# Where the modulation's partial sums are folded: from TensorE to GpSimd and VectorE

## The chip, the core and the metric

The kernel runs on one NeuronCore of a Trainium2 chip, as one program. The metric is the device time of one execution in microseconds; of several runs the median is given. The engines are named as the profile names them: PE (TensorE matmuls), PEld (TensorE's weight loads, which overlap PE), DVE (VectorE), ACT (ScalarE), POOL (GpSimd) and SP (SyncE, which here only issues DMAs).

## The reference, cut to what matters

The network is a diffusion transformer of two layers on 256 latent tokens and 256 context tokens of width 1024, one retention layer and one neighbourhood-attention layer, each followed by an MLP. Every layer is modulated: a vector `c` (and `c_ctx` for the context) is multiplied by a 1024 x 6144 matrix, and the product is cut into six pieces, shift, scale and gate for the mixer and for the MLP.

```
silu_c = silu(c); silu_cc = silu(c_ctx)
for i in range(2):
    mod   = silu_c  @ ada_w[i] + ada_b[i]        # 1024 -> 6144, for the latents
    mod_c = silu_cc @ ada_w[i] + ada_b[i]        # the same for the context
    sh1, sc1, g1, sh2, sc2, g2 = split(mod, 6)
    h = x * (1 + sc1) + sh1
    y = mixer(h)                                 # retention (i=0), neighbourhood attention (i=1)
    x = layer_norm(ALPHA * x + g1 * y)
    h = x * (1 + sc2) + sh2
    x = layer_norm(ALPHA * x + g2 * mlp(h))      # and the same for the context where i=0
```

The change touches only how `mod` and `mod_c` are finished, for all pieces but the first shift and scale of layer 0.

## The kernel before, in words

All large products run on PE with float32 operands split in a high and a low part (`hi`, `lo`), three matmuls for each product. The work is one long sequence of stages: an opening (projection of the first retention head, together with the first modulation, which PE computes itself), four retention heads (0 to 3), the first MLP in two halves, then the second layer: neighbourhood attention and its MLP. Weights are streamed from DRAM by SP into the pool `rawp` (tiles `raw`, `rawa` for the modulation's matrix; four buffers for both), ACT rounds them (`hi`), DVE subtracts (`lo`).

The later modulation is a background task, `bg_stream`. It has ten parts, named (layer, which modulation, part): parts 0 and 1 are two halves of shift and scale ("columns"), part 2 is the gate. In order: (0,0,2), (0,1,0), (0,1,1), (0,1,2), (1,0,0), (1,0,1), (1,0,2), (1,1,0), (1,1,1), (1,1,2). For each part eight pieces of the matrix are loaded, DVE multiplies each with a column of silu(c) and adds up per partition (`weigh`, in `strips` in layer 0's parts and in `acc` later), and `folded` reduces that on DVE with a transposing reduction into a small tile `red`: 128 partitions by 32 columns for each of the `nt` token kinds. What is left are four groups of 32 partitions that have to be added. `nt` is 2 where the context needs its own modulation, and 1 in the parts (1,0,2) and (1,1,0) to (1,1,2).

That last addition is the subject. It is put in the list `due` and run by `flush` at the next background step: `ada_columns` for parts 0 and 1, `ada_gate` for part 2. Before the change PE does it: a matmul of `red` with the constant `fold` (a 128 x 32 matrix that is one where the partition modulo 32 equals the column), into a bank of PSUM that the program calls `pada`. For columns there are four such matmuls, one for each quarter of the output partitions, and DVE adds the bias on the way out into `mods`. For a gate there is one; DVE transposes the result, adds the bias, which POOL has fetched by DMA into the tile `gate`, and POOL writes the row to DRAM (`grow`) by DMA, from where SP or ACT load it later broadcast over the partitions (`load_gate`, tile `G`). The scratch `gate` is one of the eight tiles of the pool `scp` (`scr`).

`mods` is read by `fold`, which combines it on POOL with the layer norm's weights (`AB`, three small instructions). The first reader of (0,1) is the end of head 3, that of (1,0) the end of the first MLP, that of (1,1) the end of the attention.

Instructions are written in program order, but the Tile framework's scheduler sets the order on each engine from its own costs, except where `InOrder` pins an engine (`pe.on`, `dve.on` and so on). POOL is mostly free; it also does the row statistics' power (`rstd`), the products `gs`, the accumulation into the residual `R` and the issue of its own DMAs. Every engine runs its instructions strictly in the order shown, so an instruction that waits holds up all behind it.

Of the kernel before, what the change touches and what calls it, by code (L numbers as in the profile page):

```python
# [10 lines left out]
F32 = mybir.dt.float32  # L11
# [6 lines left out]
P = 128  # L18
# [86 lines left out]
def kernel(  # L105
# [23 lines left out]
    pe, act, dve, pool, sp = (  # L129
        InOrder(tc, getattr(nc, e), e in PIN)  # L130
        for e in ("tensor", "scalar", "vector", "gpsimd", "sync")
    )
# [3 lines left out]
    smp = ec(tc.tile_pool(name="smp", bufs=4))  # L136
# [15 lines left out]
    def nm(s):  # L152
        uid[0] += 1
        return f"{s}_{uid[0]}"

    def bank(s="ps"):
        return psp.tile([P, 512], F32, tag="ps", name=nm(s))
# [5 lines left out]
    def scr(s, dt=F32):  # L163
        return scp.tile([P, 512], dt, tag="scr", name=nm(s))
# [138 lines left out]
    def cv(name, p0=0, p1=P):  # L303
        o, w = CONST_COLS[name]
        if o < NC0:
            return cst0[p0:p1, o : o + w]
        return cst1[p0:p1, o - NC0 : o - NC0 + w]
# [59 lines left out]
    mods = {}  # L367
# [62 lines left out]
    def folded(red, acc, t, c0, n):  # L430
# [3 lines left out]
            axis=mybir.AxisListType.X, op=ALU.add, apply_transpose=True,  # L434
        )

    def ada_columns(l, w, red, c0, nt):

        pr = bank("pada")
        for j in range(4):  # L440
            pe.matmul(
                pr[32 * j : 32 * j + 32, 0 : 8 * nt],
                lhsT=cv("fold"),
                rhs=red[:, :nt].rearrange("p t (k j) -> p j (t k)", j=4)[:, j],
                start=True,
                stop=True,
                tile_position=(0, 32 * j),
            )
        dve.tensor_add(
            out=mods[l, w][:, :, c0 : c0 + 4, :],  # L450
            in0=(
                pr[:, 0:16].rearrange("p (t s k) -> p s k t", t=2, s=2)
                if nt == 2
                else pr[:, 0:8].rearrange("p (s k) -> p s k", s=2).unsqueeze(3).broadcast_to([P, 2, 4, 2])
            ),
            in1=acol[:, COLUMNS.index((l, w)), :, c0 : c0 + 4].unsqueeze(3).broadcast_to([P, 2, 4, 2]),
        )

    def ada_gate(l, w, red, nt):

        tmp = scr("gate")[0:32, :]
        bias, tot, row = tmp[:, 0:32], tmp[:, 64 : 64 + 32 * nt], tmp[:, 128 : 128 + 32 * nt]
        g = (3 * w + 2) * D
        pool.dma_start(out=bias, in_=ada_b[l][g : g + D].rearrange("(b i) -> b i", i=32))
        pr = bank("pada")
        pe.matmul(
            pr[0:32, 0 : 32 * nt], lhsT=cv("fold"), rhs=red[:, :nt].rearrange("p t b -> p (t b)"),
            start=True, stop=True, tile_position=(0, 0),
        )
        dve.transpose(out=tot, in_=pr[0:32, 0 : 32 * nt])  # L470
        dve.tensor_add(
            out=row.rearrange("p (t i) -> p t i", t=nt), in0=tot.rearrange("p (t i) -> p t i", t=nt),
            in1=bias.unsqueeze(1).broadcast_to([32, nt, 32]),
        )
        for t in range(nt):
            pool.dma_start(
                out=grow[l, w][t].rearrange("(b i) -> b i", i=32), in_=row[:, 32 * t : 32 * t + 32]
            )
# [26 lines left out]
    def bg_stream():  # L505
# [13 lines left out]
        for step, (l, w, part, offs, n) in enumerate(plan):  # L519
# [28 lines left out]
            if n == KC - 1:  # L548
                if part < 2:
                    due.append(lambda a=(l, w, red, 4 * part, nt): ada_columns(*a))  # L550
                else:
                    due.append(lambda a=(l, w, red, nt): ada_gate(*a))
# [324 lines left out]
    def part_v(k, a, b):  # L877
# [8 lines left out]
        out=lgn[:, 0], in_=ret_decay[0].rearrange("(o d) h -> o (d h)", o=1).broadcast_to([P, 8])  # L886
# [19 lines left out]
    w = ws[0]  # L906
# [98 lines left out]
    for h in range(RH):  # L1005
# [9 lines left out]
        else:  # L1015
# [15 lines left out]
            for u in range(4):  # L1031
                ((wh, wl),) = take(1)
                for t in range(4):
                    for kk in range(2):
                        k = 2 * u + kk
# [72 lines left out]
        for t in range(4):  # L1108
            po = bank("po")
            scs = list(range(4)) if t < 2 else [2, 3]  # L1110
            for i, sc in enumerate(scs):
                a, b = S[sc]
# [8 lines left out]
                out=on, in0=po[:], scalar1=mv[:, 0:1], scalar2=r[:], op0=ALU.subtract, op1=ALU.mult  # L1121
# [51 lines left out]
        else:  # L1173
# [11 lines left out]
            def proj(t, half):  # L1185
                return gated(tok_mm(t, half, wus[half]), t, half, G1)
# [4 lines left out]
            def turn(t):  # L1191
                return [mod_pt(xns[t], half) for half in range(2)]
# [16 lines left out]
            tmp = proj(1, 1)  # L1209
# [10 lines left out]
            tmp = proj(2, 1)  # L1220
# [56 lines left out]
    for hf in range(2):  # L1277
# [65 lines left out]
        for half in range(2):  # L1343
# [39 lines left out]
            def settle(t):  # L1383

                add_to(t, 1, gated(pb[t], t, 1, G2), dve)
                stat(t, 1)
                return moments(t)
# [14 lines left out]
            m = settle(0)  # L1402
# [5 lines left out]
            m = settle(1)  # L1408
            mm2(2, 4, held[0])
            p = turn(0)  # L1410
# [7 lines left out]
            m = settle(2)  # L1418
            mm2(3, 4, held[0])
            p = turn(1)  # L1420
# [299 lines left out]
    m = settle(3)  # L1720
# [123 lines left out]
    n = NS - 1  # L1844
# [373 lines left out]
```

## Time and profile before

| | us |
|---|---|
| median of 3 runs | 1178.11 |
| lowest, highest run | 1176.97, 1178.76 |
| the profiled execution | 1180.28 |
| its span in the profile | 1178.2 |
| PE busy, share of the span | 1168.4, 99% |
| DVE busy | 846.6, 72% |
| ACT busy | 482.0, 41% |
| POOL busy | 212.9, 18% |
| granted TensorE clock, mean | 0.998 |

The span runs from the first to the last instruction; 2.1 us of the profiled execution's time lie outside it. PE's busy time counts overlapping instructions once and its ends are modelled; so the starts of successive matmuls say more than their lengths. In the rows of a timeline the columns are start, busy time, engine, line, operation, output<-inputs, shapes, how many instructions are merged in the row, and in brackets how long the engine had been idle and what ended it. Almost all rows have line 84, which is the helper that issues each instruction; tiles' names tell them apart. The profile shows each of the kernel's folding matmuls as two records, since their operands are plain float32.

### The profile page before, as it was taken

How to read it: one execution, taken by the hardware profiler on the slowest of the kernel's cores; microseconds unless marked ns; L12 is line 12 of the kernel's file. 1: busy time of each engine (PE TensorE's matmuls, PEld its weight loads, DVE VectorE, ACT ScalarE, POOL GpSimd, SP SyncE). 2: the span in 40 equal slices, each digit the busy share in tenths (PEclk: the TensorE clock that was granted, in tenths of full speed). 3: DMA queues.
4: the chain of work that ended last, by engine and by line, in shares of the span. 5: the costliest groups of instructions: out<-in, count | busy, mean ns of one | idle time of the engine just before them, and what ended most of it. 6: DMA issues, size and time to landing. Idle time of an engine off the chain costs nothing.

```text
span 1178.2 us, 17591 instructions
## 1 busy us (share of the span) xinstructions
PE 1168.4 (99%) x6743; PEld 985.0 (84%) x6743; DVE 846.6 (72%) x1351; ACT 482.0 (41%) x819; POOL 212.9 (18%) x364
## 2 busy tenths in 40 slices
PE   9999999999999999999999999999999999999997
PEld 7788888888888889888888888889888878999886
DVE  3887677777888787757767675678576688876446
ACT  3643332232323246341113332137466576665341
POOL 0103001000200241770203000223344430000001
PEclk9999999999999999999999999999999999999999
DMA  9942544544355426756556665647244434765661
GB/s 279 273 143 93 158 146 146 156 144 143 126 170 170 149 59 218 184 110 212 179 183 211 202 207 187 192 140 212 76 144 126 123 123 151 224 197 189 230 213 38
DMA packets 140115, 195.10 MB, mean 166 GB/s; under 512 B 9936, under 2 KB 81136, under 8 KB 140032
## 3 DMA queue, kind: packets, MB, share of 16 engines
q1 hardware_dynamic: 131904, 182.03, 49.6%
q0 software_dynamic: 6976, 9.39, 3.9%
q10 hardware_dynamic: 1152, 2.56, 0.8%
q8 instruction: 53, 0.87, 0.3%
q14 instruction: 30, 0.25, 0.1%
HBM read 189.12 MB, written 5.75 MB: 165 GB/s over the span
## 4 chain that ended last, share of the span: by engine, by line
PE 97%; DVE 1%; ACT 1%; issue 0%; DMA 0%; POOL 0%; DVEq 0%; ACTq 0%
PE p L84 44%; PE pq L84 8%; PE pv L84 8%; PE pg L84 7%; PE pw L84 7%; PE pn L84 5%; PE pnv L84 4%; PE po L84 3%; PE ppt L84 2%; PE pnw L84 1%; PE pS L84 1%; PE pav L84 1%; PE pada L84 1%; PE pqk L84 1%; PE pt L84 1%; PE p1t L84 1%
## 5 line engine op out<-in xcount | busy, mean ns | idle before, releaser
L84 ACT CAST hi<-raw 128x1024 fp32r<-128x1024 f32 (+2 forms) x228 | 232.7, 1032 | 310.9 <-PE p L84 124.3
L84 DVE TENSOR_TENSOR lo<-raw,hi 128x1024 fp32r<-128x1024 f32 (+2 forms) x228 | 274.0, 1213 | 106.2 <-ACT hi L84 105.7
L84 PE MATMUL p<-hi,hid 128*128 128x512 f32 (+1 forms) x780 | 239.0, 386 | 0.0
L84 PEld LDWEIGHTS p<-hi,hid 128*128 128x128 f32 x780 | 145.7, 188 | 29.5
L84 PE MATMUL p<-hTh,lo 128*128 128x256 f32 (+1 forms) x512 | 166.9, 329 | 0.0
L84 PE MATMUL p<-hTl,hi 128*128 128x256 f32 (+1 forms) x512 | 166.9, 329 | 0.0
L84 PE MATMUL p<-hTh,hi 128*128 128x256 f32 (+1 forms) x512 | 164.0, 330 | 0.0
L84 PE MATMUL p<-lo,hid 128*128 128x512 f32 (+1 forms) x390 | 150.5, 386 | 0.0
L84 DVE SCALAR_TENSOR_TENSOR acc<-rawa,scol,acc 128x1024 f32<-128x1024 f32 x56 | 74.6, 1342 | 65.5 <-DMA rawa<-in_ada_w_dram 65.5
L84 PEld LDWEIGHTS p<-hTh,lo 128*128 128x128 f32 x512 | 96.4, 188 | 8.8
L84 PEld LDWEIGHTS p<-hTl,hi 128*128 128x128 f32 x512 | 96.5, 188 | 8.6
L84 PEld LDWEIGHTS p<-hTh,hi 128*128 128x128 f32 x512 | 95.1, 190 | 8.7
L84 PEld LDWEIGHTS p<-lo,hid 128*128 128x128 f32 x390 | 73.3, 188 | 14.5
L84 DVE SCALAR_TENSOR_TENSOR strips<-rawa,scol,strips 128x512 f32<-128x512 f32 x112 | 78.6, 762 | 0.0
L84 ACT CAST hid<-r 128x256 fp32r<-128x256 f32 (+1 forms) x64 | 31.9, 500 | 106.9 <-DVE r L84 106.9
L84 POOL TENSOR_TENSOR rstd<-rstd,misc 128x1 f32<-128x1 f32 x28 | 19.1, 685 | 213.6 <-DVE rstd L84 212.6
L84 POOL TENSOR_TENSOR R<-R,acc 128x512 f32<-128x512 f32 x16 | 25.9, 1635 | 169.8 <-DVE acc L84 169.7
L84 ACT ACTIVATE s<-s,mn 128x512 f32<-128x512 f32 x64 | 45.5, 713 | 22.0 <-DVE mn L84 22.0
L84 PE MATMUL pw<-hi,oh 128*128 128x512 f32 x128 | 51.0, 398 | 0.0
L84 PE MATMUL pg<-hi,hTh 128*128 128x512 f32 x128 | 50.6, 395 | 0.0
L84 PE MATMUL pw<-hi,ol 128*128 128x512 f32 x128 | 50.0, 390 | 0.0
L84 PE MATMUL pg<-hi,hTl 128*128 128x512 f32 x128 | 49.9, 390 | 0.0
(238 smaller groups left out, 2279.8 us busy)
## 6 DMA issues: line engine op xcount, KB each, us to landing
raw<-in_mlp_w_dram SPq DMA_DIRECT2D x128, 512.0 KB, 4.4
rawa<-in_ada_w_dram SPq DMA_DIRECT2D x80, 512.0 KB, 3.9
raw<-in_ret_w_in_dram SPq DMA_DIRECT2D x42, 512.0 KB, 4.0
raw<-in_nat_w_in_dram SPq DMA_DIRECT2D x24, 512.0 KB, 4.5
rawq<-in_ada_w_dram SPq DMA_DIRECT2D x16, 512.0 KB, 6.1
raw<-in_ret_w_o_dram SPq DMA_DIRECT2D x16, 512.0 KB, 3.5
bias<-rpb_rows POOLq DMA_DIRECT2D x32, 128.0 KB, 2.9
raw<-in_nat_w_o_dram SPq DMA_DIRECT2D x8, 512.0 KB, 3.9
```

Of the source, the lines that this page charges most:

```text
L84: r = f(*args, **kwargs)
```

## The change

The four groups of 32 partitions are added by two copies and two additions (`strip_sums`): partitions 64 to 127 are copied beside partitions 0 to 63 and added, then 32 to 63 beside 0 to 31. For columns POOL does it, four more POOL copies spread the sums to the four quarters of `mods`, and a POOL addition adds the bias. For gates DVE does it, and its transpose then reads `red` and no PSUM. The scratch (`far`, `gate`) moves from `scr` into the tile `row` of the opening, of which there is one.

```diff
+    def strip_sums(red, nt, far, eng):
+        far = far[:, : 32 * nt].rearrange("p (t b) -> p t b", t=nt)
+        for n in (64, 32):
+            eng.tensor_copy(out=far[0:n], in_=red[n : 2 * n, :nt])
+            eng.tensor_add(out=red[0:n, :nt], in0=red[0:n, :nt], in1=far[0:n])
+        return red[0:32, :nt]
+
     def ada_columns(l, w, red, c0, nt):
-        pr = bank("pada")
+        far = smp.tile([P, 256], F32, tag="row", name=nm("far"), bufs=1)
+        tot = strip_sums(red, nt, far, pool).rearrange("p t (s k j) -> p j s k t", s=2, j=4)
+        m = mods[l, w][:, :, c0 : c0 + 4, :]
         for j in range(4):
-            pe.matmul(
-                pr[32 * j : 32 * j + 32, 0 : 8 * nt],
-                lhsT=cv("fold"),
-                rhs=red[:, :nt].rearrange("p t (k j) -> p j (t k)", j=4)[:, j],
-                start=True, stop=True, tile_position=(0, 32 * j),
-            )
-        dve.tensor_add(
-            out=mods[l, w][:, :, c0 : c0 + 4, :],
...
+            pool.tensor_copy(
+                out=m[32 * j : 32 * j + 32], in_=tot[:, j] if nt == 2 else tot[:, j].broadcast_to([32, 2, 4, 2])
+            )
+        pool.tensor_add(
+            out=m, in0=m,
             in1=acol[:, COLUMNS.index((l, w)), :, c0 : c0 + 4].unsqueeze(3).broadcast_to([P, 2, 4, 2]),
         )

     def ada_gate(l, w, red, nt):
-        tmp = scr("gate")[0:32, :]
+        tmp = smp.tile([P, 256], F32, tag="row", name=nm("gate"), bufs=1)
...
-        pr = bank("pada")
-        pe.matmul(
-            pr[0:32, 0 : 32 * nt], lhsT=cv("fold"), rhs=red[:, :nt].rearrange("p t b -> p (t b)"),
-            start=True, stop=True, tile_position=(0, 0),
-        )
-        dve.transpose(out=tot, in_=pr[0:32, 0 : 32 * nt])
+        dve.transpose(out=tot, in_=strip_sums(red, nt, tmp[:, 192:], dve).rearrange("p t b -> p (t b)"))
```

On PE the ten places lose their matmuls and nothing else changes its place. On DVE and POOL the scheduler orders some instructions anew. Three places follow, with before first.

DVE in head 1, between the projection of the values and the scores, where the gate (0,0,2) is finished. `red_953` is the part's reduced sum, `lo_1607` a weight's low part, `vl` the low part of the head's values read out of the banks `pv`, `strips` the running sums of the next part:

```order
L84 TENSOR_TENSOR lo_1575<-raw_1572,hi_1574 128x1024
L84 TENSOR_TENSOR lo_1607<-raw_1604,hi_1606 128x1024
L84 TENSOR_TENSOR vl_1495<-pv_1496,vh_1494 128x512
L84 TENSOR_TENSOR vl_1495<-pv_1497,vh_1494 128x512
L84 TENSOR_TENSOR vl_1495<-pv_1498,vh_1494 128x512
L84 STREAM_TRANSPOSE gate_1634<-pada_1636 32x64
L84 TENSOR_TENSOR gate_1634<-gate_1634 32x64
L84 TENSOR_SCALAR strips_118<-rawa_1566,scol 128x512
```

```order
L84 TENSOR_TENSOR lo_1575<-raw_1572,hi_1574 128x1024
L84 COPY gate_1634<-red_953 64x64
L84 TENSOR_TENSOR red_953<-red_953,gate_1634 64x64
L84 COPY gate_1634<-red_953 32x64
L84 TENSOR_TENSOR red_953<-red_953,gate_1634 32x64
L84 STREAM_TRANSPOSE gate_1634<-red_953 32x64
L84 TENSOR_TENSOR gate_1634<-gate_1634 32x64
L84 TENSOR_SCALAR strips_118<-rawa_1566,scol 128x512
```

The gate's work moved ahead of `lo_1607` and of the four `vl`, which now stand behind it and behind four instructions on `strips`.

DVE in head 3, where the gate (0,1,2) is finished; `po` are the head's outputs in PSUM, `bs`, `mv` and `on` their statistics and normalized values:

```order
L84 TENSOR_REDUCE red_2877<-strips_118 128x16
L84 TENSOR_REDUCE red_2877<-strips_119 128x16
L84 BN_STATS bs_3398<-po_3385 128x6
L84 BN_AGGR mv_3400<-bs_3398 128x2
L84 TENSOR_SCALAR on_3405<-po_3385,mv_3400,rstd_3402 128x512
```

```order
L84 TENSOR_REDUCE red_2887<-strips_118 128x16
L84 TENSOR_REDUCE red_2887<-strips_119 128x16
L84 COPY gate_3580<-red_2887 64x64
L84 TENSOR_TENSOR red_2887<-red_2887,gate_3580 64x64
L84 COPY gate_3580<-red_2887 32x64
L84 TENSOR_TENSOR red_2887<-red_2887,gate_3580 32x64
L84 STREAM_TRANSPOSE gate_3580<-red_2887 32x64
L84 TENSOR_TENSOR gate_3580<-gate_3580 32x64
L84 BN_STATS bs_3408<-po_3395 128x6
```

Six small instructions now stand between the reduction and the head's first statistics; before, the transpose and the last addition stood some twenty instructions later, behind the matmul.

POOL in head 3, from the end of head 2 on; `AB` is the fold of (0,1), `grow` the gate row's two DMAs, `rstd` the first power of head 3's statistics:

```order
L84 TENSOR_TENSOR gs_2454<-sg_2724,gs_2454 128x512
L84 TENSOR_TENSOR AB_3578<-mod_101,lnT 128x16 x2
L84 TENSOR_TENSOR AB_3578<-AB_3578,mod_101 128x16
L84 TENSOR_SCALAR rstd_3402<-mv_3400 128x1
L84 TENSOR_TENSOR rstd_3402<-rstd_3402,misc 128x1
```

```order
L84 COPY far_2875<-red_2339 64x64
L84 TENSOR_TENSOR red_2339<-red_2339,far_2875 64x64
L84 COPY far_2875<-red_2339 32x64
L84 TENSOR_TENSOR red_2339<-red_2339,far_2875 32x64
L84 COPY mod_101<-red_2339 32x2x8 x4
L84 DMA gate_3580<-in_ada_b_dram 32x32
L84 TENSOR_TENSOR mod_101<-mod_101,acol 128x2x8
L84 TENSOR_TENSOR AB_3590<-mod_101,lnT 128x16 x2
L84 TENSOR_TENSOR AB_3590<-AB_3590,mod_101 128x16
L84 DMA grow_111<-gate_3580 32x32 x2
L84 TENSOR_SCALAR rstd_3412<-mv_3410 128x1
L84 TENSOR_TENSOR rstd_3412<-rstd_3412,misc 128x1
```

The columns' sums stand before the fold, and the bias' DMA and the gate row's DMAs moved ahead of the statistics; before, these DMAs stood after the head's last products `gs`.

More of the change, by code (lines that the diff above doesn't have):

```diff
@@ L435, in folded @@
         )
+    def strip_sums(red, nt, far, eng):
[4 more added lines that the diff above has]
+        return red[0:32, :nt]
     def ada_columns(l, w, red, c0, nt):
-        pr = bank("pada")
+        far = smp.tile([P, 256], F32, tag="row", name=nm("far"), bufs=1)
+        tot = strip_sums(red, nt, far, pool).rearrange("p t (s k j) -> p j s k t", s=2, j=4)
+        m = mods[l, w][:, :, c0 : c0 + 4, :]
         for j in range(4):
-            pe.matmul(
-                pr[32 * j : 32 * j + 32, 0 : 8 * nt],
-                lhsT=cv("fold"),
-                rhs=red[:, :nt].rearrange("p t (k j) -> p j (t k)", j=4)[:, j],
-                start=True,
-                stop=True,
-                tile_position=(0, 32 * j),
-            )
-        dve.tensor_add(
-            out=mods[l, w][:, :, c0 : c0 + 4, :],
[L451 to L455, printed above, removed]
+            pool.tensor_copy(
+                out=m[32 * j : 32 * j + 32], in_=tot[:, j] if nt == 2 else tot[:, j].broadcast_to([32, 2, 4, 2])
+            )
+        pool.tensor_add(
+            out=m, in0=m,
             in1=acol[:, COLUMNS.index((l, w)), :, c0 : c0 + 4].unsqueeze(3).broadcast_to([P, 2, 4, 2]),
@@ L459, in ada_gate @@
     def ada_gate(l, w, red, nt):
-        tmp = scr("gate")[0:32, :]
-        bias, tot, row = tmp[:, 0:32], tmp[:, 64 : 64 + 32 * nt], tmp[:, 128 : 128 + 32 * nt]
+        tmp = smp.tile([P, 256], F32, tag="row", name=nm("gate"), bufs=1)
+        bias, tot, row = (tmp[0:32, 64 * i : 64 * i + 32 * n] for i, n in enumerate((1, nt, nt)))
         g = (3 * w + 2) * D
         pool.dma_start(out=bias, in_=ada_b[l][g : g + D].rearrange("(b i) -> b i", i=32))
-        pr = bank("pada")
-        pe.matmul(
-            pr[0:32, 0 : 32 * nt], lhsT=cv("fold"), rhs=red[:, :nt].rearrange("p t b -> p (t b)"),
-            start=True, stop=True, tile_position=(0, 0),
-        )
-        dve.transpose(out=tot, in_=pr[0:32, 0 : 32 * nt])
+        dve.transpose(out=tot, in_=strip_sums(red, nt, tmp[:, 192:], dve).rearrange("p t b -> p (t b)"))
         dve.tensor_add(
```

## Prediction

> **What bounds the kernel.** I read the page's busy shares first, then the chain that ended last, then what PE waited for:
>
> ```profile
> PE 1168.4 (99%) x6743; PEld 985.0 (84%) x6743; DVE 846.6 (72%) x1351; ACT 482.0 (41%) x819; POOL 212.9 (18%) x364
> PE 97%; DVE 1%; ACT 1%; issue 0%; DMA 0%; POOL 0%; DVEq 0%; ACTq 0%
> PE pq L84 <- DVE still L84: 1.2, 1, 1.2
> PE pq L84 <- DVE hTh L84: 0.4, 1, 0.4
> PE pt L84 <- ACT xn L84: 0.2, 1, 0.2
> ```
>
> The reader is to see that three things agree: PE is busy nearly throughout, the chain back from the last instruction runs on PE for 97% of the span, and the waits of PE's matmuls (last three rows: total, times, longest) come to 1.8 us. So the end is set by the sum of PE's own starts, and a microsecond taken off PE is a microsecond of the end, as long as nobody else is then late. The prediction has two halves: how long PE really spends on the ten folds, and whether POOL and DVE, which take the work, hold PE up anywhere.
>
> **What PE gives back.** PE's share cannot be read from the matmuls' lengths, since they overlap. I take starts: from the last ordinary matmul ahead of a fold to the second one behind it, because the first one behind it still starts its successor late. PE's timeline at the columns (0,1,0) (first of six) and (1,1,1) (last), and at the four gates in order of time:
>
> ```profile
> 256.87 0.39 PE L84 MATMUL pv<-lo,hTh 128*128 128x512 f32 x1
> 257.10 0.39 PE L84 MATMUL pv<-hi,hTl 128*128 128x512 f32 x1
> 257.42 0.26 PE L84 MATMUL pada<-red,cst 128*32 128x16 f32 x8
> 257.61 0.50 PE L84 MATMUL pv<-hi,hTh 128*128 128x512 f32 x1
> 257.95 0.39 PE L84 MATMUL pv<-lo,hTh 128*128 128x512 f32 x1
> ...
> 729.03 0.39 PE L84 MATMUL p<-hi,hid 128*128 128x512 f32 x1
> ...
> 729.87 0.39 PE L84 MATMUL p<-lo,hid 128*128 128x512 f32 x1
> ...
> 171.72 0.39 PE L84 MATMUL pv<-hi,hTl 128*128 128x512 f32 x1
> ...
> 172.49 0.28 PE L84 MATMUL pS<-qkl,qkh 128*128 128x256 f32 x1
> ...
> 410.56 0.39 PE L84 MATMUL pg<-hi,hTl 128*128 128x512 f32 x1
> 410.88 0.30 PE L84 MATMUL pada<-red,cst 128*32 128x64 f32 x2
> ...
> 411.45 0.39 PE L84 MATMUL pw<-lo,oh 128*128 128x512 f32 x1
> ...
> 657.48 0.39 PE L84 MATMUL p<-hTh,lo 128*128 128x512 f32 x1
> ...
> 658.32 0.39 PE L84 MATMUL p<-hTl,hi 128*128 128x512 f32 x1
> ...
> 772.96 0.39 PE L84 MATMUL p<-hi,hid 128*128 128x512 f32 x1
> ...
> 773.79 0.39 PE L84 MATMUL p<-lo,hid 128*128 128x512 f32 x1
> ```
>
> What the same step takes without a fold is seen where head 2 goes from its values to its scores, which is the passage at 172 us with nothing between:
>
> ```profile
> 273.84 0.39 PE L84 MATMUL pv<-hi,hTl 128*128 128x512 f32 x1
> 274.06 0.28 PE L84 MATMUL pS<-qkh 128*128 128x256 f32 x1
> 274.18 0.28 PE L84 MATMUL pS<-qkl,qkh 128*128 128x256 f32 x1
> ```
>
> A new bank and new weights cost no gap there: the 512-wide step is 0.22, the 256-wide one 0.12. Between two 512-wide ones the step is 0.23 (256.87 to 257.10), and two of them 0.45.
>
> - Columns with two token kinds, 16 elements wide, four calls: 257.95 - 257.10 = 0.85, less 0.45, is 0.40 each: 1.60 us.
> - Columns with one kind, 8 wide, two calls: 729.87 - 729.03 = 0.84, less 0.45, 0.39 each: 0.78 us.
> - Gates: 172.49 - 171.72 = 0.77 less 0.34 (274.18 - 273.84), 0.43; 411.45 - 410.56 = 0.89 less 0.45, 0.44; 658.32 - 657.48 = 0.84 less 0.45, 0.39; 773.79 - 772.96 = 0.83 less 0.45, 0.38. Together 1.64 us.
>
> The sum is 4.0 us. Eight records cost as much as two, so it is going into and out of a fold that costs, and removing one saves all of it.
>
> TensorE: Matmul & The Clock Gate, section "Wait — 56ns, not 53.3ns?", a page of the Trainium skill, states a floor of about 25 ns from one small matmul's start to the next. By that floor alone the 56 records would be worth an estimated 1.4 us and not 4.0; the rows differ, since most of the 0.85 lies ahead of and behind the eight records (0.32 from 257.10 to 257.42, 0.34 from 257.61 to 257.95), and the measurement decides.
>
> **One place where a wait gets shorter too.** PE's only late wait is the first transpose after head 3, for ACT's `xn`. Its chain begins with DVE reading `pw` behind the fold at 410.88; there DVE also waited for the bias:
>
> ```profile
> 412.62 2.69 DVE L84 TENSOR_TENSOR lo<-raw,hi 128x1024 fp32r<-128x1024 f32 x1 [1.16 <-ACT hi L84]
> 415.63 0.21 DVE L84 TENSOR_TENSOR gate<-gate 32x64 f32<-32x64 f32 x1 [0.33 <-DMA gate<-in_ada_b_dram]
> 423.49 1.09 PE L84 MATMUL pt<-cst,xn 128*128 128x128 f32 x8 [0.24 <-ACT xn L84]
> ```
>
> The gate's two instructions leave this place, so the statistics can follow PE's 0.44 us earlier end. Between nothing and the whole 0.24 of the wait I take 0.1 us.
>
> **What POOL and DVE take on.** The prices, from the tiles' and groups' rows nearest in shape:
>
> ```profile
> L84 DVE COPY row<-pada x9: 290/425/425, 6.9 to 53.3; 128x256 f32<-128x256 f32 x7, 128x128 f32<-128x128 f32 x2
> 172.37 0.24 DVE L84 STREAM_TRANSPOSE gate<-pada 32x64 f32<-32x64 f32 x1 [0.28 <-PE pada L84]
> 172.65 0.21 DVE L84 TENSOR_TENSOR gate<-gate 32x64 f32<-32x64 f32 x1
> L84 POOL COPY pt<-s 128x32 f32<-128x32 f32 x64 | 15.5, 246 | 79.4 <-ACT s L84 78.8
> L84 POOL TENSOR_TENSOR AB<-mod,lnT 128x16 f32<-128x16 f32 x6 | 2.5, 434 | 29.0 <-DVE mod L84 24.3 <-DVE aff L84 4.7
> L84 POOL DMA_DIRECT2D grow<-gate x6 | 3.2, 529 | 115.1 <-DVE gate L84 115.1
> ```
>
> A call of columns is nine POOL instructions, six copies at 0.25 and three additions at 0.43: 2.8 us, six times 17 us on an engine that is busy 213 of 1178. The trace has no POOL copy across partitions; the bounds are 0.25 and 0.43 for it too, so 2.8 to 3.9 us a call, and I take 2.8. A gate is four more DVE instructions of 0.2 to 0.29 each; with the transpose and the addition that is 1.3 to 1.6 us, some four times 1 us more on DVE.
>
> Where could these stand in front of something PE needs? In head 1 the six DVE instructions and the four on `strips` move ahead of the four `vl`. DVE idled there before the next weight was rounded, and the `vl` wait for ACT's `vh`, which trails PE, so the move fills idle time: I cost it at nothing. In head 3 they stand ahead of the first statistics, and POOL's two `grow` DMAs ahead of the first `rstd`:
>
> ```profile
> 390.30 1.29 DVE L84 TRANSPOSE_TENSOR_REDUCE red<-strips 128x16 f32<-128x512 f32 x2
> 393.74 0.70 DVE L84 BATCH_NORM_STATS2 bs<-po 128x6 f32<-128x512 f32 x1 [2.15 <-PE po L84]
> 394.74 0.22 POOL L84 TENSOR_SCALAR rstd<-mv 128x1 f32<-128x1 f32 x1 [65.44 <-DVE mv L84]
> 407.74 0.68 DVE L84 TENSOR_TENSOR ol<-pT,oh 128x512 fp32r<-128x512 f32 x1
> ```
>
> DVE has 2.15 us there, waiting for PE's `po`, and needs at most 1.6, so the gate is done at 393.2. POOL issues two DMAs in 1.06 us, until 394.3, and `rstd` can start at 394.74 as before. This is the tightest place, and behind it comes more cover: `ol` at 407.74 ends at 408.42, and PE reads it at 411.11 or, with the fold gone, 410.7, 2.3 us later. Before the fold's `AB` POOL has no reader until the MLP. In the first MLP the columns (1,0,1) now precede the four additions into `R`:
>
> ```profile
> 607.60 2.36 DVE L84 TRANSPOSE_TENSOR_REDUCE red<-acc 128x32 f32<-128x1024 f32 x2
> 618.58 7.09 POOL L84 TENSOR_TENSOR R<-R,acc 128x512 f32<-128x512 f32 x4 [38.16 <-DVE acc L84]
> ```
>
> From 609.96 to 618.58 are 8.6 us; the columns (2.8 to 3.9), the bias' DMA (0.5) and the three of `AB` (1.3) need 4.6 to 5.7. Hidden as well. What could lengthen these is that DVE and POOL hinder each other: `lo` at 412.62 took 2.69 us while POOL multiplied `gs`, against 1.21 as the mean of its group.
>
> ```profile
> L84 DVE TENSOR_TENSOR lo<-raw,hi 128x1024 fp32r<-128x1024 f32 (+2 forms) x228 | 274.0, 1213 | 106.2 <-ACT hi L84 105.7
> ```
>
> SBUF — State Buffer, section "SBUF: two separate sides", in the Trainium skill, speaks against the change here: POOL and a DVE instruction with two SBUF inputs exclude each other for a whole instruction; the trace agrees in that row. Counted against the sum, DVE would lose no more than POOL's new 17 to 23 us, over six places; it waits over 100 us for ACT's `hi` in that same group, so the late instructions are mostly ones that PE needs much later. I take nothing, with 1 us as the upper bound of what reaches PE. The scratch in `row` adds waits of one gate or column call for the one before it, which lie tens of microseconds apart, and gives `scr` a tile back; nothing either way.
>
> **Sum.** 4.0 + 0.1 = 4.1 us less: the span 1178.2 becomes 1174.1, the profiled execution's 1180.28 about 1176.2. That execution lies 2.2 us above the median of the runs; from the median 1178.11 the forecast is 1174.0 us. About 0.2%, 2.4 us, is what a measurement of this kernel can tell from no change; 4.1 us is 0.35%.
>
> **Rivals.**
>
> 1. PE's gap is partly given back. For it speaks that PE is so close to its suppliers (`hTh`, `xn`, `lo`) that starts 0.4 us earlier may meet operands that are not earlier; against it that PE's waits sum to 1.8 us, so slack is usual. If 2.0 to 4 us of waits appear, or if only the matmuls' own starts were saved, the time is 1176.0 to 1178.1, around 1176.9: no change that can be told. Chance 0.15.
>
> 2. Slower: head 3's queues. If the six DVE instructions or the bias they wait for hold the first statistics, `on`, `gs`, the transposes and `ol` slide with them. It decides only beyond the cover: 2.3 us behind `ol` and then 4.1 + 2.4 us of gain to eat, so the first statistics would have to be 8.8 us late, at 402.5. At 0.29 us an instruction six cannot do it; they would have to take 1.8 us each, as if POOL shut DVE out every time. The time then would be 1180.5 or more. Chance 0.05.
>
> 3. A larger gain: DVE no longer waits on PE for the folds' results, and waits of PE's weight loads behind it shrink. It could add 1 to 2 us: 1172 to 1173. Chance 0.08.
>
> The change does do what it says: all 28 matmuls are gone from PE's order and no other row of PE has moved.
>
> **How the numbers follow.** The likeliest, PE's 4.0 us and no new wait over 1 us, has 0.72 and gives 1173.5 to 1175.5. Faster by over 0.2% is it and rival 3, 0.80; no change 0.15; slower 0.05. The range from 1172.3 to 1177.2 takes rival 3 and two thirds of rival 1 in.
>
> **What would show it.** In the profile after, PE should have 56 records fewer, and at the ten places steps of 0.23. PE's waits should stay at about 2 us; POOL's busy time should rise by 17 to 23 us, DVE's change by under 4. In head 3 the first statistics should still wait for `po`. The forecast is wrong if PE's list of waits has a new row of 1 us or more, most likely for `pT`, `ol` or `lo` in head 3, or if the gaps around the folds remain as gaps of another cause.

## The result, and the profile after

The changed kernel took 1175.92 us in the median (1173.7 to 1176.43, 8 runs) beside 1177.88 us for the kernel before on the same chip (1176.97 to 1180.19, 8 runs): a ratio of 0.9976, 95% interval 0.9966 to 0.9985, that is 2.8 us or 0.24% less, with 1.8 to 4.0 us as the interval. Timed again in two later sets it had 0.9969 twice (0.9955 to 0.9983, and 0.9957 to 0.9981): 3.7 us. The forecast was 4.1 us, and 1174.0 us. The profiled execution took 1176.32 us, its span is 1174.4.

The page after: busy shares, the chain that ended last by engine, and PE's waits (total, times, longest):

```profile
PE 1161.8 (99%) x6687; PEld 980.7 (84%) x6687; DVE 848.4 (72%) x1361; ACT 481.1 (41%) x819; POOL 235.1 (20%) x418
PE 74%; DMA 12%; DVE 8%; issue 3%; ACT 2%; POOL 0%; DVEq 0%; ACTq 0%
PE p L84 <- DVE lo L84: 2.1, 2, 1.7
PE pq L84 <- DVE still L84: 1.2, 1, 1.2
PE pc L84 <- DMA brow<-in_ada_b_dram: 0.8, 1, 0.8
PE pq L84 <- DVE hTh L84: 0.4, 1, 0.4
```

The 56 records are gone (6743 to 6687), DVE gained 1.8 us and POOL 22.2. But the chain has changed its look: it ran on PE for 97% before, and here for 74%, with 12% on DMAs and 8% on DVE. That is what one late operand does: the chain goes back through the first row of the waits, PE for `lo`, and from there follows the stream of modulation weights (`rawa`, then DVE's `acc`) for about a fifth of the span. From 716 us to the last weighing that chain holds hardly anything but the stream's loads, 3.5 to 4.9 us each, and its weighings, mostly 1.3 us: there the stream goes at its own pace. This row is new, it is over 1 us, and by the prediction's own words it would make the forecast wrong. The folds' places themselves look as foreseen. PE's timeline at the columns (0,1,0) and at the gate (0,1,2), where the fold used to stand behind the second `pv` row and behind the `pg` row:

```profile
257.38 0.39 PE L84 MATMUL pv<-lo,hTh 128*128 128x512 f32 x1
257.60 0.39 PE L84 MATMUL pv<-hi,hTl 128*128 128x512 f32 x1
257.83 0.39 PE L84 MATMUL pv<-hi,hTh 128*128 128x512 f32 x1
...
410.23 0.39 PE L84 MATMUL pg<-hi,hTl 128*128 128x512 f32 x1
410.46 0.39 PE L84 MATMUL pw<-hi,oh 128*128 128x512 f32 x1
410.68 0.39 PE L84 MATMUL pw<-lo,oh 128*128 128x512 f32 x1
```

Steps of 0.22 to 0.23 throughout. To see where the time went beyond that, I match every PE matmul of the two traces and take its start after less its start before. This *shift* adds up over the program, and only its steps count:

| where | step of the shift, us | |
|---|---|---|
| opening, to 55 us | +0.95 | `pc` waits 0.8 for `brow` |
| ten folds, each from the third matmul ahead to the sixth behind | -4.14 | -0.43, -0.42, -0.42, -0.45, -0.42, -0.42, -0.40, -0.40, -0.40, -0.40 |
| first transposes after head 3, 423 us | -0.29 | the wait for `xn` is gone |
| last weights of the first MLP, 766 to 772 us | +2.75 | PE waits for `lo` |
| neighbourhood attention, 880 us | -0.4 | |
| second MLP's first product, 1013 to 1082 us | -2.65 | matmuls 113.3 ns apart, not 117.8 |

The folds gave 4.14 us, and then 3.7 us of unforeseen losses met 3.3 us of unforeseen gains. That a sum comes out near its forecast is no proof that its terms did, and most of the experiments ask which of these rows belong to the change.

The row at 766 us, on DVE and then on PE, after:

```profile
763.10 1.28 DVE L84 SCALAR_TENSOR_TENSOR acc<-rawa,scol,acc 128x1024 f32<-128x1024 f32 x1 [0.35 <-DMA rawa<-in_ada_w_dram]
764.91 1.23 DVE L84 TRANSPOSE_TENSOR_REDUCE red<-acc 128x32 f32<-128x1024 f32 x1
...
766.74 0.18 DVE L84 COPY gate<-red 64x32 f32<-64x32 f32 x1
766.95 1.23 DVE L84 TENSOR_TENSOR lo<-raw,hi 128x1024 fp32r<-128x1024 f32 x1
768.10 0.18 DVE L84 TENSOR_TENSOR red<-red,gate 64x32 f32<-64x32 f32 x1
...
769.07 3.48 DVE L84 TENSOR_TENSOR lo<-raw,hi 128x1024 fp32r<-128x1024 f32 x3
...
768.23 0.50 PE L84 MATMUL p<-lo,hid 128*128 128x512 f32 x1 [1.70 <-DVE lo L84]
770.33 0.50 PE L84 MATMUL p<-lo,hid 128*128 128x512 f32 x1 [0.43 <-DVE lo L84]
```

These `lo` are the low parts of the four weights that are held for the end of the first MLP. DVE waits for the last weights of the modulation stream (0.35), weighs and reduces them, and only then comes to the first low part; five of the gate (1,1,2)'s six small instructions stand between it and the next. Two things can be late here, the stream and the gate.

### The profile page after: what moved, and what is told of

It is laid out like the page before. It is cut to its first block, busy times and chain, and to the rows that moved or that the text cites. A ratio compares the mean times of both kernels' runs of the same rounds, so it can differ in the third digit from the quotient of the medians.

```text
span 1174.4 us, 17544 instructions
## 1 busy us (share of the span) xinstructions
PE 1161.8 (99%) x6687; PEld 980.7 (84%) x6687; DVE 848.4 (72%) x1361; ACT 481.1 (41%) x819; POOL 235.1 (20%) x418
## 4 chain that ended last, share of the span: by engine, by line
PE 74%; DMA 12%; DVE 8%; issue 3%; ACT 2%; POOL 0%; DVEq 0%; ACTq 0%
PE p L84 23%; DMA rawa<-in_ada_w_dram 11%; PE pq L84 8%; PE pv L84 8%; PE pw L84 7%; PE pg L84 7%; PE pn L84 4%; DVE acc L84 4%; PE pnv L84 4%; PE po L84 3%; DVE lo L84 3%; PE pnw L84 1%; PE ppt L84 1%; PE pS L84 1%; PE pav L84 1%
## 5 line engine op out<-in xcount | busy, mean ns | idle before, releaser
L84 PE MATMUL pw<-lo,oh 128*128 128x512 f32 x128 | 49.8, 389 | 0.0
```

The source lines that it names most:

```text
L84: r = f(*args, **kwargs)
```

## The experiments

In what follows *last weighing* is the start on DVE of the stream's last `acc<-rawa` (763.10 above), and *loss at the held weights* the step of PE's shift against before from 767 to 772 us. Times are medians, with the ratio to the kernel before and its interval.

**Both kernels once more, unedited.** The pair tells what a second execution looks like.

> The changed kernel once more, without an edit. It asks two things of the trace. First, the second MLP's first product (matmuls of 256 columns, 1013 to 1082 us) had a pitch of 117.8 ns before and 113.3 ns after at a clock of 1.00, worth 2.6 us that nothing in the change explains. If the placement of buffers sets it, it is 113.3 again here; if it differs from one execution to the next, it may be either value. Second, PE's new wait of 1.7 + 0.4 us for the low parts of the held weights at 768 to 770 us: my theory (PE, 2.9 us earlier, has caught up with the stream of modulation weights, which is paced by its DMAs) expects it again, 1.5 to 2.7 us in all; if it was an accident of one DMA it is under 0.5. Time: 1174 to 1176.5.

> The kernel before once more, without an edit, as the other half of the same two questions. Placement: pitch 117.8 again at 1013 to 1082 us. Execution: either value. No wait of PE for the low parts of the held weights at 769 us by either theory, since PE comes there 2.9 us later. Time: 1177 to 1179, a ratio of 1.000 within 0.001.

The changed kernel: 1175.76 us, 0.9969 (0.9955 to 0.9983). The kernel before: 1180.16 us, where 1177 to 1179 was expected, 1.0006 (0.9994 to 1.0018). PE's timeline near 1040 us, one matmul of 256 columns and the ninth behind it: the changed kernel in its first profile and in this one, then the kernel before in its first and in this one.

```profile
1039.74 0.28 PE L84 MATMUL p<-hTl,hi 128*128 128x256 f32 x1
...
1040.76 0.28 PE L84 MATMUL p<-hTl,hi 128*128 128x256 f32 x1
```

```profile
1039.73 0.28 PE L84 MATMUL p<-hTl,hi 128*128 128x256 f32 x1
...
1040.79 0.28 PE L84 MATMUL p<-hTl,hi 128*128 128x256 f32 x1
```

```profile
1039.79 0.28 PE L84 MATMUL p<-hTl,hi 128*128 128x256 f32 x1
...
1040.85 0.28 PE L84 MATMUL p<-hTl,hi 128*128 128x256 f32 x1
```

```profile
1039.79 0.28 PE L84 MATMUL p<-hTl,hi 128*128 128x256 f32 x1
...
1040.81 0.28 PE L84 MATMUL p<-hTl,hi 128*128 128x256 f32 x1
```

Nine steps take 1.02 and 1.06 us in the changed kernel, 1.06 and 1.02 before: the pitch changed places, 113.3 then 117.8 ns in the one (over the whole stage), 117.8 then 113.3 in the other. It is one of these two values through the whole stage, in every profile of this study (117.8 in four of fourteen), and placement is out. So the 2.65 us belong to the execution, not to the change; with a granted clock of 1.00 in all of them, what chooses the value stays open.

At the held weights my theory missed. In this profile PE does not wait at all, and the loss is 0.00. On DVE, and on PE the matmul that waited 1.70 us above:

```profile
759.37 1.28 DVE L84 SCALAR_TENSOR_TENSOR acc<-rawa,scol,acc 128x1024 f32<-128x1024 f32 x1 [0.45 <-DMA rawa<-in_ada_w_dram]
763.22 1.23 DVE L84 TENSOR_TENSOR lo<-raw,hi 128x1024 fp32r<-128x1024 f32 x1
...
765.83 0.39 PE L84 MATMUL p<-lo,hid 128*128 128x512 f32 x1
```

The last weighing came 3.7 us earlier than in the first profile, the low part was done at 764.45, and PE read it at 765.83: 1.4 us of slack. The last weighings of all kernels with the stream in its place, the experiments below among them. Where PE waited, the time at which it was due is that of the first profile of before with the shift just ahead of the place:

| kernel | last weighing | PE due at the first low part | loss |
|---|---|---|---|
| before, first profile | 762.92 | 769.33 | |
| before, again | 763.36 | 769.74 | none |
| folds doubled | 763.15 | 770.89 | 0.00 |
| columns only | 759.32 | 767.61 | 0.00 |
| gates only | 761.38 | 768.09 | 0.00 |
| changed, first profile | 763.10 | 766.38 | 2.75 |
| changed, again | 759.37 | 765.83 | 0.00 |
| changed, third profile | 759.65 | 765.63 | 0.05 |
| last gate later | 762.04 | 766.00 | 1.04 |
| columns on DVE | 766.88 | 769.79 | 3.97 |

In some executions the stream follows PE's earlier start to the end (759.3 to 759.7); in the first one its weighings ran up to 1.9 us ahead of before until 630 us and had lost this lead by 713 us. The first low part is ready 4.7 to 4.8 us after the last weighing where the gate's sum is on PE or done later, and 5.1 to 5.2 us where it is on DVE in between. So PE waits in the three rows where it is due less than that after the last weighing (3.3, 4.0 and 2.9 us), and in no other (6.0 us or more): in two of them because the stream is late for a PE that is 3 us early, in the third because the stream is later still.

Without this wait the shift of the changed kernel ends at -4.30 us here, at the same pitch as before. That it comes so near the folds' -4.14 is chance: -0.25 at the first transposes and -0.37 at 880 us stand beside a new loss of 0.46 in head 2, where DVE waited for the DMA of `xin` and PE then for DVE's `ol`:

```profile
315.50 0.69 DVE L84 SCALAR_TENSOR_TENSOR R<-xin,R 128x512 f32<-128x512 f32 x1 [1.45 <-DMA xin<-in_x_dram]
...
318.17 0.50 PE L84 MATMUL pw<-hi,ol 128*128 128x512 f32 x1 [0.17 <-DVE ol L84]
```

This loss comes in four of the ten profiles of kernels with moved sums (0.26 to 0.60) and in none of the four with all folds on PE, though DVE waited for `xin` up to 1.0 us there too. The third profile of the changed kernel has neither this wait nor, but for 0.05, the one at the held weights, and ends at -4.48.

**One half each.**

The first has `ada_gate` as it was, the second `ada_columns`:

```diff
-        dve.transpose(out=tot, in_=strip_sums(red, nt, tmp[:, 192:], dve)...)
+        pr = bank("pada")
+        pe.matmul(pr[0:32, 0 : 32 * nt], lhsT=cv("fold"), rhs=red[:, :nt]...)
+        dve.transpose(out=tot, in_=pr[0:32, 0 : 32 * nt])
```

```diff
-        tot = strip_sums(red, nt, far, pool)...
...
-        pool.tensor_add(out=m, in0=m, ...)
+        pr = bank("pada")
+        for j in range(4):
+            pe.matmul(pr[32 * j : 32 * j + 32, 0 : 8 * nt], lhsT=cv("fold"), ...)
+        dve.tensor_add(out=mods[l, w][:, :, c0 : c0 + 4, :], in0=pr..., ...)
```

> Only the columns' sums leave PE (to POOL); the four gates are folded on PE as before. By the prediction's own terms PE is earlier by 6 x 0.40 = 2.4 us, read as the shift of PE's starts against before in steps of 0.4 at the six places, and the gates' folds stay. DVE's list near the held weights is that of before, PE comes 2.4 us earlier there, so the wait for the held weights' low parts is at most 0.7 us. Time, without the second MLP's pitch: 2.4 us under before, 1.7 to 2.4. Rival (one half carries the whole gain): 0 to 0.8 or 3.5 to 4 us here.

> Only the gates' sums leave PE (to DVE); the six columns are folded on PE as before. By the prediction's terms PE is earlier by 0.43 + 0.44 + 0.39 + 0.38 = 1.6 us, and by up to 0.3 more at the first transpose after head 3, where the shift then shows a step at 423 us (it stays in the kernel with only the columns moved). At the held weights PE comes 1.5 us earlier: a wait of 0 to 0.7 us there. Time without the second MLP's pitch: 1.2 to 1.9 us under before. Rival as in the other half: 0 to 0.5 or 3.5 to 4 us.

Columns only: 1175.56 us, 0.9980 (0.9970 to 0.9990). Gates only: 1176.70 us, 0.9994 (0.9984 to 1.0004). In the shift, the steps at the ten places in order of time were 0, -0.42, -0.42, 0, -0.42, -0.42, +0.01, -0.40, -0.40, 0 (sum 2.46) and -0.43, 0, 0, -0.45, 0, 0, -0.39, 0, 0, -0.40 (sum 1.67). The halves add up to 4.13, the whole to 4.14: the terms are separate, and each sits where it was put. The time of the gates alone cannot be told from no change, which a gain of 1.67 us, 0.14%, would hardly be. A part of the expectation fell: with only the columns moved, the shift also has a step of -0.24 at 423 us, though the gates' two instructions were still there. The wait for `xn` was 0.24 in the first profile of before and 0.6 in the second: it differs by execution. The step at 880 us does not. It is -0.3 to -0.4 in all ten profiles of kernels with moved sums, the halves among them, and nothing (0.02 and 0.01) in the two other profiles that have PE's instructions as before. But it is also -0.33 with the folds doubled (next experiment), so it goes with the program and not with the sums. PE runs small `pqk` matmuls there; why they go faster stays open.

**What a fold costs.** The kernel before, each fold's matmuls issued twice.

```diff
-        for j in range(4):
+        for j in [0, 1, 2, 3] * 2:
             pe.matmul(pr[32 * j : 32 * j + 32, 0 : 8 * nt], ...
...
+        for _ in range(2):
             pe.matmul(pr[0:32, 0 : 32 * nt], ...
```

> The kernel before with every fold's matmuls issued twice into the same bank (112 records in place of 56), the sums unchanged. My reading of the trace: the 0.40 us of a fold is mostly going into and out of it (0.09 us longer ahead of it, 0.11 behind it), and the four matmuls of four column groups start 7 ns apart; then a second set costs 0.05 to 0.10 us, 0.5 to 1.0 us over ten folds. Rival, a floor of about 25 ns from one start to the next (the Trainium skill's page on TensorE): 8 more records cost 0.20 us in a column fold, 1.3 us in all with the gates'. Rival, the cost is per matmul in proportion: 4 us in all, time 1184. Read from the step at each fold, not from the time, which runs to run moves more.

1178.50 us, 1.0004 (0.9996 to 1.0013). PE's timeline at the columns (0,1,0) and the gate (0,1,2):

```profile
257.61 0.39 PE L84 MATMUL pv<-hi,hTl 128*128 128x512 f32 x1
257.92 0.33 PE L84 MATMUL pada<-red,cst 128*32 128x16 f32 x16
258.18 0.50 PE L84 MATMUL pv<-hi,hTh 128*128 128x512 f32 x1
258.51 0.39 PE L84 MATMUL pv<-lo,hTh 128*128 128x512 f32 x1
...
411.19 0.39 PE L84 MATMUL pg<-hi,hTl 128*128 128x512 f32 x1
411.51 0.41 PE L84 MATMUL pada<-red,cst 128*32 128x64 f32 x4
411.85 0.50 PE L84 MATMUL pw<-hi,oh 128*128 128x512 f32 x1
```

The gap ahead of a fold is what it was (0.31 to 0.32), the one behind it too (258.18 to 258.51, 0.33), and the columns' fold itself grew from 0.19 to 0.26. Over ten folds 56 more records added 0.73 us to the shift (0.5 to 1.0 expected), 0.06 in a column fold and 0.06 to 0.13 in a gate's. So the reading holds: most of the 0.40 is going in and out. In the traces the four matmuls on four column groups start 7 ns apart. By the floor of TensorE: Matmul & The Clock Gate, section "Wait — 56ns, not 53.3ns?", a page of the Trainium skill, eight more starts would take an estimated 0.20 us, three times the 0.06 that they took here; the measurement decides.

**The stream two steps earlier, after and before.**

```diff
             if hf:
                 bg(2 + fp % 2)
+            elif fp >= 6:
+                bg()
```

> The changed kernel with the stream of modulation weights started two steps earlier, in the last two blocks of the first product of the first MLP half, so that it ends about two steps (10 us) before the held weights. Stream theory: PE's wait of 2.1 us for the held weights' low parts is gone, the 2.7 us of shift lost at 769 us are kept, time 1171.5 to 1174, unless the two extra loads make the product's own weights late around 500 us. Rival (the six small DVE instructions of the last gate between the low parts are what costs): they also move away with the stream, so the same gain; the next kernel tells these two apart. Rival (the loss was an accident of one execution): as the unedited kernel, within 0.5 us.

> The kernel before, folds on PE, with the stream of modulation weights started two steps earlier. Theory: the early stream pays only where PE has caught up with the stream's end; before, PE comes 3 to 4 us later to the held weights and finds their low parts ready (slack 1.7 us in its profiles), so nothing changes: no shift of PE's starts over 0.5 us around 769 us, time within 1 us of before. Rival (an early stream is worth something by itself, by relieving the later DMAs): 1 to 3 us under before.

After: 1173.88 us, 0.9959 (0.9944 to 0.9974); the last weighing at 750.17, the first low part 4.6 us ahead of PE, a loss of 0.00, and no new wait elsewhere. Before: 1177.61 us, 0.9999 (0.9989 to 1.0009), its last weighing at 750.56, no step at the held weights. So the early stream alone is worth nothing that the time or PE's shift shows, and after the change it takes the stream's end out of PE's way. By time alone its gain over the unedited kernel (1175.76 in the same set) is not settled, since the intervals overlap.

**The last gate later.** The six DVE instructions of (1,1,2) go behind the first normalization after the held weights.

```diff
+            last_gate, due[:] = list(due), []
             A, B = fold(0, 1, 1, 0)
...
             whiten(0, m)
+            due[:] = last_gate
+            flush()
```

> The changed kernel with the last gate's (1,1,2) six DVE instructions put behind the first normalization after the held weights, so that nothing small stands between the low parts. Stream theory: the first low part still comes late, since DVE waits for the last modulation weights ahead of it; its wait shrinks from 1.7 to about 1.4 us and only the second one (0.4) goes: a gain of 0.4 to 0.8 us, time 1174 to 1175.5. Rival (the gate's instructions on DVE are the cause): both waits go, a gain of 2 to 2.7 us, time 1171.5 to 1174.

1173.87 us, 0.9954 (0.9941 to 0.9967). DVE and PE there:

```profile
762.04 1.36 DVE L84 SCALAR_TENSOR_TENSOR acc<-rawa,scol,acc 128x1024 f32<-128x1024 f32 x1 [0.27 <-DMA rawa<-in_ada_w_dram]
765.65 4.61 DVE L84 TENSOR_TENSOR lo<-raw,hi 128x1024 fp32r<-128x1024 f32 x4
...
766.91 0.50 PE L84 MATMUL p<-lo,hid 128*128 128x512 f32 x1 [0.74 <-DVE lo L84]
```

The last weighing fell between the others' values, at 762.04, and PE waited 0.74 us, once (loss 1.04). The first low part was ready 4.8 us after it (5.1 with the gate in between), and the second wait is gone, as the stream theory has it. So of the 2.75 us lost in the first profile the gate's instructions have, by an estimate from these profiles, about 1.0: 0.3 of the first wait (5.1 less 4.8), and the second one, 0.7 in the shift (770.33 against 768.23 + 1.36, the step between two such matmuls without a wait: 765.83 to 767.19 in the repeat). The other 1.7 are the stream. The gain in time, 1.9 us by the medians, is larger than the 0.4 to 0.8 that I expected, and again the intervals overlap.

**The stream one step later.** It was meant as the forced case.

```diff
-                bg(2 + fp % 2)
+                bg(2 + fp % 2 * (fp < 7))
```

> The changed kernel with one step of the stream taken from the last block of the first product of the second MLP half, so that it ends one step later. Stream theory: the last weighing starts 2.6 to 5.4 us later than in the neighbour (a step of the stream takes 5.2 to 5.8 us there in the profiles so far), and PE waits for the held weights' low parts by that much more, 2.5 to 7 us in all: time 2 to 5 us over the neighbour, so as slow as the kernel before or slower. Rival (the order of the small instructions matters, not the stream's end): the same wait as the neighbour within 1 us.

1176.00 us, 0.9977 (0.9963 to 0.9991), 0.6 us over its neighbour; loss 0.92. The expectation of 2.5 to 7 us failed. The last weighing did come 3.2 us later than in the neighbour:

```profile
759.90 1.20 DVE L84 TENSOR_TENSOR lo<-raw,hi 128x1024 fp32r<-128x1024 f32 x1
762.82 1.28 DVE L84 SCALAR_TENSOR_TENSOR acc<-rawa,scol,acc 128x1024 f32<-128x1024 f32 x1 [1.72 <-DMA rawa<-in_ada_w_dram]
...
766.61 3.48 DVE L84 TENSOR_TENSOR lo<-raw,hi 128x1024 fp32r<-128x1024 f32 x3
...
767.87 0.50 PE L84 MATMUL p<-lo,hid 128*128 128x512 f32 x1 [0.63 <-DVE lo L84]
```

But the step taken from the stream let the first held weight pass it: its low part now stands ahead of the last weighing, so only the second was late, by 0.63 us. I had moved the stream and not looked at what it would swap places with. That a late stream makes PE wait rests on three profiles with the last weighing at 762 to 763 us (losses 2.75, 1.04, 0.92) beside two at 759.5 without loss, and on the next experiment's (766.88, loss 3.97), not on this test's size.

**The columns on DVE too.** All nine instructions of a column call go from POOL to DVE.

```diff
-        tot = strip_sums(red, nt, far, pool)...
+        tot = strip_sums(red, nt, far, dve)...
...
-            pool.tensor_copy(out=m[32 * j : 32 * j + 32], ...)
-        pool.tensor_add(out=m, in0=m, ...)
+            dve.tensor_copy(out=m[32 * j : 32 * j + 32], ...)
+        dve.tensor_add(out=m, in0=m, ...)
```

> The changed kernel with the columns' nine small instructions on DVE in place of POOL, so that all ten sums are DVE's. At 0.2 us each that is 1.8 us a call, 11 us more on DVE in six places, POOL's busy time falls to that of before. Theory (sums anywhere off PE are hidden while the stage has idle time on the engine that takes them): the same time as the changed kernel within 0.5 us, PE's shift in the same steps of 0.4. Rival (DVE has no room in the MLP stages, where it trails PE): a new wait of PE for hid, lo or acc of 0.5 us or more right behind a column call, time 1 to 4 us over the changed kernel.

1176.15 us, 0.9989 (0.9977 to 1.0001). PE's ten steps are the same (4.13), DVE was busy 8.7 us more than after, and no wait appeared at a column call. But the loss at the held weights was 3.97 us, with the last weighing at 766.88. The profile can't say that DVE's load did it: in this execution the opening ran 4.4 us late (last section), PE had made up nearly all of it by 767 us and the stream had not. Inconclusive; POOL is at least no worse a place.

**Early stream and late gate together, with the unedited kernel beside it.**

> The changed kernel with both: the stream of modulation weights two steps earlier, and the last gate's six DVE instructions behind the first normalization. From the profiles so far the last weighing on DVE starts at 759.4 to 763.4 us in every kernel, whatever PE does, and the first held low part is ready 4.7 to 5.1 us later; with the stream early it started at 750.2. So no wait of PE for a low part at the held weights in any execution, and PE's shift of 4.0 us against the kernel before is kept. Time: 1172.5 to 1175, 4.0 to 5 us under before, 0 to 2 us under the unedited changed kernel of the same call. Rival (the two extra loads hurt the first product elsewhere): a new wait of PE over 0.5 us between 480 and 520 us.

> The changed kernel without an edit, as the neighbour of the other two of this call. Wait for the held low parts: 0 to 2.1 us, by whether the stream's last weighing on DVE starts at about 759.5 or 763. Pitch of the 256-wide matmuls: 117.8 or 113.3 ns. Time 1174 to 1176.5.

Together: 1173.69 us, 0.9958 (0.9943 to 0.9973); the third run of the changed kernel: 1175.40 us, 0.9969 (0.9957 to 0.9981). No wait of PE for `lo` in either profile. With the edit the first held low part was done at 760.1, 5.7 us ahead of PE. The end of the shift is -4.74 and -4.48 us, at the same pitch. The two edits remove the chance of the wait; the 1.7 us between the medians are plausible for that, and not proved. This version beats the kernel before by 5.0 us (3.2 to 6.7).

## Why the prediction came out right

**PE gives back 4.0 us.** Held: 4.14 in the first profile, the repeat, the third and the combination alike, and 4.13 with the columns on DVE. By halves: columns 2.46 (2.38 foreseen), gates 1.67 (1.64). The extra 0.1 lies in the matmuls behind a fold, which I had measured over a shorter stretch.

**0.1 us at the first transposes.** Not settled. The wait vanished (-0.29), and it is gone in all ten profiles of kernels with moved sums. But it is gone as well with the gates still folded on PE, and in the kernel before with the early stream, where every fold is on PE (-0.24); in the three other profiles with all folds on PE it is 0.24, 0.6 and 0.7.

**POOL's price.** Mis-sized. I took 2.8 us a call, 17 in all; POOL gained 22.2, 3.7 us a call, near the upper bound of 3.9. POOL's groups after, with count, busy time and mean in ns:

```profile
L84 POOL COPY mod<-red 32x16 f32<-32x16 f32 x24 | 7.5, 312 | 1.1
L84 POOL COPY far<-red 64x64 f32<-64x64 f32 (+3 forms) x12 | 7.3, 606 | 180.5 <-DVE red L84 152.6 <-issue 27.5
L84 POOL TENSOR_TENSOR red<-red,far 64x64 f32<-64x64 f32 (+3 forms) x12 | 6.2, 513 | 1.0
L84 POOL TENSOR_TENSOR mod<-mod,acol 128x16 f32<-128x16 f32 x6 | 1.4, 226 | 0.5
```

The `far` copies across partitions took 0.61 us and not 0.25; the other prices are off by less. It cost nothing, since no PE wait follows a column call.

**DVE's gates, and head 3.** Held. DVE gained 1.8 us (under 4 foreseen). Head 3's gate, first statistics and POOL after:

```profile
391.35 0.19 DVE L84 COPY gate<-red 64x64 f32<-64x64 f32 x1
...
392.56 0.21 DVE L84 TENSOR_TENSOR gate<-gate 32x64 f32<-32x64 f32 x1
393.40 0.70 DVE L84 BATCH_NORM_STATS2 bs<-po 128x6 f32<-128x512 f32 x1 [0.63 <-PE po L84]
393.07 1.03 POOL L84 DMA_DIRECT2D grow<-gate  x2 [61.62 <-DVE gate L84]
394.41 0.22 POOL L84 TENSOR_SCALAR rstd<-mv 128x1 f32<-128x1 f32 x1 [0.31 <-DVE mv L84]
```

The six instructions took 1.42 us (1.3 to 1.6 foreseen). DVE's idle time shrank from 2.15 to 0.63 us and still ended with PE's `po`, and `rstd` waited for `mv`, not for the two DMAs. Behind it the prediction misread a row: 411.11 is where PE first reads `oh`, and its first matmul with `ol` started at 411.68 in before, so this row's cover was 0.6 us more than I counted. No profile has a wait for `ol` in head 3. The order in head 1 cost nothing as well: in the repeat PE's shift is -0.42 us behind the fold at 172 us and ahead of the one at 257.

**No new wait over 1 us: this step failed, in the profile after, though not in every execution.** I looked for the tightest place among the gates in the heads and named `pT`, `ol` or `lo` in head 3. What I did not ask is which suppliers can keep a pace of their own. PE's whole gain piles up until 766 us, and by then it must be matched by everyone who doesn't wait for PE. The modulation stream, which ends just ahead of the held weights and in this execution did not follow PE, had 1.7 us of slack there in the profile of before (first low part done at 767.65, read at 769.33), and 2.96 us of gain met it. I also costed the last gate, whose six instructions stand among these low parts, with the others at nothing: about 1.0 us. The rival of a gain partly given back, at 0.15, is what this execution shows at that place. That its time lay within the range all the same was luck: a gain of 2.65 us that isn't the change's stood beside the loss. In how many of the runs without a profile the loss occurs isn't known; of three profiles of the changed kernel one has it. Rival 3, a gain of 1 to 2 us more, isn't seen in the shift beyond the -0.25 and -0.37 above.

**The level.** From 4.1 us the measured gain differs by 0.4 us in the two later sets and by 1.3 in the first, just outside that interval's end of 4.0. Single executions of one kernel lie several us apart (1172.71 to 1180.51 in the repeat of the changed one) from causes, some of them in the last section, that have nothing to do with the change, so an agreement closer than 1 us would be luck.

## What to carry to other kernels

Small matmuls in the middle of a dense stream cost mostly what it takes to go in and out of them (0.4 us here for 2 or 8 records, and 0.06 more for 16), so read a fold's price from ordinary matmul to ordinary matmul, and remove it whole. When the bound engine gets faster by pieces, add the pieces up along the program and hold the sum at each place against the slack of suppliers that can run at their own pace; one whose slack is smaller gives part of the gain back, in the executions in which it does not follow. And take a second profile of both kernels before explaining a difference between two: of the six rows of the first table the folds and in part the held weights were the change's, the opening and the pitch came and went by execution, the transposes are not settled, and the row at 880 us came with the new program for a reason not found.

## What the runs showed of the hardware

The 256-wide matmuls ran 113.3 or 117.8 ns apart through a whole stage, by execution, at a granted clock of 1.00. In two executions (stream early, and columns on DVE) the opening also ran slower, 4.4 to 4.6 us by 18 us into the program. PE's timeline at the same four matmuls, with the stream early and then in the repeat of the changed kernel, and the stretch from 9 to 18 us (busy time and count of PE, PEld, DVE, ACT and POOL, then granted clock, DMA share and GB/s):

```profile
14.69 1.91 PE L84 MATMUL pv<-hi,hTh 128*128 128x512 f32 x4
...
9.00:18.00 9.00, 8.91 (x58) 6.51 (x61) 3.08 (x7) 2.77 (x5) 0.00 (x0) 1.00 1.19 303
```

```profile
11.34 1.08 PE L84 MATMUL pv<-hi,hTh 128*128 128x512 f32 x4
...
9.00:18.00 9.00, 8.62 (x72) 6.66 (x73) 5.24 (x11) 3.74 (x7) 0.00 (x0) 1.00 1.18 303
```

From the first of these four 512-wide starts to the matmul behind them it took 1.71 us in the one (to 16.40) and 0.92 in the other (to 12.26), nearly twice as long, with the granted clock shown as 1.00 in both: the clock's column does not show this slow stretch, and only the starts do. Whether the clock or something else slowed it isn't shown. What sets off either, and why the modulation stream falls back in some executions between 630 and 713 us, wasn't found.
